# Sparse gate weights by accumulating scatters instead of one-hot products, and finer steps for attention units and scan chunks

## Chip, cores and metric

The kernel runs on one core of one Trainium2 chip. The metric is the device time of one execution in microseconds (us); most executions of this kernel agree within 0.3%. The engines are named as the profile names them: PE (matrix products; PEld is its loading of weights), DVE (vector), ACT (scalar), POOL (GpSimd, which here issues the indirect DMAs) and SP (which here issues nearly all other DMAs).

## What is computed

One layer of a hybrid decoder on 1024 tokens of width 1024, in float32. The mixer has three branches (a chunked state-space scan, dilated attention in three groups of heads, attention into 256 memory tokens), each gated and merged. Then comes the part that the change is about, a retrieval of single-neuron experts:

```
top, pos = top_k(cand, 16)               # per token: 8 heads x 16 = 128 of 16384 experts
idx  = take_along_axis(cidx, pos)
gate = softmax(top)                      # 128 gates per token
act  = gelu(einsum('bld,blhkd->blhk', hn, expert_down[idx]))
coef = gate * act
h   += einsum('blhk,blhkd->bld', coef, expert_up[idx])
```

## The kernel before, in words

**Stages.** The tokens are worked on in two halves of 512 (four tiles of 128). Each half runs `front` (scan, attention, gated merging), `close` and `route` (which chooses each token's experts). The second half's `front` and `close` run from about 1300 to 2250 us, and the stage in which the dense tiles' products are made (the `product` stage of `dense`) runs from about 2391 us to the end.

**Two ways through the experts.** Tiles 0, 1, 4 and 5 are gathered: for each of a token's 128 experts an indirect DMA brings one row of `in_down_dram` for each of 128 tokens (`dots`, tile `rowd`, L1141; DVE multiplies it with the token, L1135), and later one row of `in_up_dram` (`ups`, tile `rowu`, L1194; PE sums four such rows at once, L1180). All indirect DMAs stand in POOL's queue. Tiles 2, 3, 6 and 7 are dense: all 16384 experts are computed for them, and the gates of those that were not chosen are zero. So a dense tile needs a table of 128 tokens by 16384 gates. `gates_of` makes it: for each four tokens, DVE compares the expert numbers with a row of 0 to 127, once for the upper 7 bits and once for the lower 7 (L1256, L1257), ACT scales one of the two one-hot matrices by the gates (L1259), PE multiplies the two (`s<-work,work`, 128x128), ACT copies the result out of PSUM (L1235), and SP writes it to the DRAM tensor `w_park` (L1238). `load_gates` (L1345) reads the table back, into `wbig`, while the product stage runs.

**What sets the order.** `main` is a generator of PE blocks. Beside it run the `sides`: generators of the retrieval (heads, dots, ups, and for tiles 2 and 3 `early_gates`), each of which goes one step when a clock of estimated PE time (`pe_us`) reaches its due time, and says how much later its next step is due (2.31 for a dot, 4.4 for an up row, 4 for a step of `early_gates`). In the second half's `front`, `early_gates` is begun after `dil_close`. Within `main`, `par` runs two generators side by side by weights: attention units (`unit`) and scan chunks (`ssd_scan`) have weight 4, the projections beside them 8 to 34, and one whole unit or chunk is one step. After that a scheduler sets the order of the instructions on each engine, which is not the order in which they were written.

**Names.** `work` and `slab` are 128x512 tiles in SBUF, `t`, `s`, `mm` and `up` tiles in PSUM, `whi` and `wlo` the upper and lower part of a weight block, `coef` and `g` hidden activations of the dense tiles.

Of the kernel before, what the change touches and what calls it, by code (L numbers as in the profile page):

```python
# [91 lines left out]
D1, D2, D3, U1, U3, U4, H1, H3, L1, L2, L3, L4, WG = 2.31, 4.4, 4.4, 4.4, 4.4, 1.76, 3.0, 5.43, 9, 4.3, 2.52, 5, 4  # L92
# [12 lines left out]
def tile_hybrid_block(ctx: ExitStack, tc: tile.TileContext, keep_d, cst_d, vec_d, row_d, pos_d, xT_d, memT_d, w_in, w_mem_kv,  # L105
# [455 lines left out]
    def ssd_scan(hf, g, dts, proj):  # L561
# [4 lines left out]
        for c in range(NT):  # L566
# [24 lines left out]
            nc.vector.tensor_tensor(out=L3, in0=L3, in1=btok[:, 128:256].unsqueeze(1).to_broadcast([P, 4, P]), op=ALU.mult)  # L591
            yp = ps(tag)
# [107 lines left out]
    def unit(hf, g, i, qT, st):  # L700

        blocks = [kv[hf, g, i]]
# [25 lines left out]
        pT = []  # L728
        for hp in range(2):
            for hh in range(2):  # L730
                h = 2 * hh + hp
                x = pr[hp][:, hh * 256:hh * 256 + nk]
                nc.scalar.activation(out=x, in_=x, func=AF.Exp, scale=0.125, bias=nm[:, h:h + 1], accum_out=st[:, 260 + h:261 + h])
            tp = ps()
# [6 lines left out]
            pT.append(dst)  # L741
        op = ps()
# [26 lines left out]
    def dil_units(hf, g, qT, other):  # L769
# [4 lines left out]
        for i in range(NT):  # L774
            unit(hf, g, i, qT, st[i])
# [18 lines left out]
    def dil_close(hf, qT, nat):  # L794
# [3 lines left out]
        for n in range(NT):  # L798
            a = work(width=264)
            unit(hf, 0, n, qT, a)  # L800
# [408 lines left out]
    w_park = dram.tile([P // KG, P, NB, KG, WT], F32, name="w_park")  # L1209

    def gates_of(d, expert, gate, alloc, ps, hot, stage_of, both=None):
# [17 lines left out]
        def product():  # L1229
# [6 lines left out]
            if t4 == WT // 4 - 1:  # L1236
                for c0, n, part in stage:
                    nc.sync.dma_start(w_park[c0 // KG:(c0 + n) // KG, :, d * (P // WT) + b].rearrange("g p k t -> p g (k t)"),  # L1238
# [27 lines left out]
    def dense(hn, dpool):  # L1266
# [78 lines left out]
        def load_gates(c):  # L1345
# [48 lines left out]
    def ssd(hf, u, last):  # L1394

        dts, proj = yield from chain(ssd_dt(hf, u), ssd_proj(hf, u, 0))
        for g in range(4):
            beside = (ssd_proj(hf, u, g + 1), 12) if g < 3 else last
            _, proj = yield from par((ssd_scan(hf, g, dts, proj), 4), beside)
        return proj  # L1400

    def attend(hf, u, mp, *more):
# [3 lines left out]
        st, q2 = yield from par((dil_units(hf, 1, q1, None), 4), (dil_project(hf, u, 2), 16))  # L1406
        _, got = yield from par((dil_units(hf, 2, q2, st), 4), (chain(dil_project(hf, u, 0), *more), MORE))
# [8 lines left out]
    def front(hf, u, before):  # L1416
# [21 lines left out]
    def early_gates():  # L1438
        def stage_of(b):
# [98 lines left out]
```

## Time and profile before

| | us |
| --- | --- |
| time before, median of 3 runs | 3897.52 (3895.51 to 3899.34) |
| the profiled execution's own time | 3877.24 |
| its span in the trace | 3875.4 |
| PE busy | 3654.6 (94%) |
| DVE busy | 2747.3 (71%) |
| ACT busy | 1497.7 (39%) |
| POOL busy | 1178.7 (30%) |

The profiled execution is 20.3 us shorter than the median of the timed runs, and 1.8 us of it lie outside the span. Issuing a DMA is counted as busy on POOL (the indirect DMAs, whose addresses it works out) and not on SP.

### The profile page before, as it was taken

How to read it: one execution, taken by the hardware profiler on the slowest of the kernel's cores; microseconds unless marked ns; L12 is line 12 of the kernel's file. 1: busy time of each engine (PE TensorE's matmuls, PEld its weight loads, DVE VectorE, ACT ScalarE, POOL GpSimd, SP SyncE). 2: the span in 40 equal slices, each digit the busy share in tenths (PEclk: the TensorE clock that was granted, in tenths of full speed). 3: DMA queues.
4: the chain of work that ended last, by engine and by line, in shares of the span. 5: the costliest groups of instructions: out<-in, count | busy, mean ns of one | idle time of the engine just before them, and what ended most of it. 6: DMA issues, size and time to landing. Idle time of an engine off the chain costs nothing. (4 is left out here: it accounts for less than half of the span.)

```text
span 3875.4 us, 53775 instructions
## 1 busy us (share of the span) xinstructions
PE 3654.6 (94%) x17696; PEld 2759.9 (71%) x17696; DVE 2747.3 (71%) x7067; ACT 1497.7 (39%) x3326; POOL 1178.7 (30%) x1081
## 2 busy tenths in 40 slices
PE   8989999999989898999898888999999999999997
PEld 5767888876766686766666666777777777777664
DVE  5764555458999879988669998986666666666432
ACT  4444444343443333555542574232223222222221
POOL 0000000000024433434244412554443344444444
PEclk9989999999999978999899999999999999999999
DMA  3223334444457767888798878998988889899997
GB/s 98 73 80 112 99 108 120 128 152 136 112 194 237 262 192 244 285 302 308 248 337 316 314 252 313 351 345 329 328 320 317 284 325 329 319 323 320 332 334 293
DMA packets 459287, 956.27 MB, mean 247 GB/s; under 512 B 46336, under 2 KB 172032, under 8 KB 459008
## 3 DMA queue, kind: packets, MB, share of 16 engines
q0 software_dynamic: 147456, 536.94, 38.8%
q1 hardware_dynamic: 311552, 415.91, 32.9%
q8 instruction: 139, 2.28, 0.2%
q14 instruction: 140, 1.15, 0.1%
HBM read 882.94 MB, written 69.73 MB: 246 GB/s over the span
## 5 line engine op out<-in xcount | busy, mean ns | idle before, releaser
L246 ACT CAST whi<-wraw 128x512 fp32r<-128x512 f32 (+2 forms) x802 | 489.9, 611 | 1233.1 <-PE mm L174 879.3
L1141 POOL DMA_INDIRECT rowd<-in_down_dram,ids x512 | 595.1, 1162 | 1070.6 <-DVE act L1135 696.2
L247 DVE TENSOR_TENSOR wlo<-wraw,whi 128x512 fp32r<-128x512 f32 (+2 forms) x802 | 540.4, 676 | 490.6 <-ACT whi L246 455.0
L174 PE MATMUL mm<-uslab,whi 128*128 128x512 f32 x2240 | 738.3, 407 | 7.1 <-ACT whi L246 2.8
L1194 POOL DMA_INDIRECT rowu<-in_up_dram,ids x448 | 498.8, 1113 | 642.1 <-PE up L1180 506.1
L174 PE MATMUL mm<-whi,coef 128*128 128x512 f32 x2048 | 672.8, 399 | 5.5 <-DVE acc L1390 5.5
L174 PE MATMUL s<-uslab,whi 128*128 128x512 f32 (+1 forms) x2080 | 656.9, 397 | 10.4 <-ACT whi L246 4.1
L1135 DVE CUSTOM_DVE_ANT_0 rowd<-rowd,rowd 128x1024 f32<-128x1024 f32 x512 | 615.4, 1217 | 35.3 <-DMA rowd<-in_down_dram,ids 35.0
L174 PEld LDWEIGHTS mm<-uslab,whi 128*128 128x128 f32 x2240 | 419.9, 192 | 101.9 <-issue 11.6
L174 PEld LDWEIGHTS s<-uslab,whi 128*128 128x128 f32 (+1 forms) x2080 | 387.7, 189 | 129.9 <-issue 33.3
L174 PEld LDWEIGHTS mm<-whi,coef 128*128 128x128 f32 x2048 | 387.9, 189 | 126.4 <-issue 22.5
L174 PE MATMUL mm<-uslab,wlo 128*128 128x512 f32 x1120 | 451.6, 405 | 6.5 <-DVE wlo L247 6.4
L174 PE MATMUL s<-uslab,wlo 128*128 128x512 f32 (+1 forms) x1040 | 412.5, 397 | 13.9 <-DVE wlo L247 13.9
L174 PE MATMUL mm<-wlo,coef 128*128 128x512 f32 x1024 | 406.4, 397 | 3.8 <-DVE wlo L247 3.8
L247 DVE TENSOR_TENSOR wlo<-coef,whi 128x512 fp32r<-128x512 f32 x200 | 138.0, 690 | 224.1 <-ACT whi L246 220.1
L246 ACT CAST whi<-coef 128x512 fp32r<-128x512 f32 x200 | 124.2, 621 | 381.2 <-PE s L174 308.4
L174 PE MATMUL mm<-slab,whi 128*128 128x512 f32 x768 | 253.6, 409 | 6.3 <-DVE slab L247 2.7
L174 PEld LDWEIGHTS mm<-uslab,wlo 128*128 128x128 f32 x1120 | 213.6, 191 | 60.6 <-DVE wlo L247 10.2
L174 PEld LDWEIGHTS s<-uslab,wlo 128*128 128x128 f32 (+1 forms) x1040 | 196.0, 188 | 63.3 <-DVE wlo L247 17.9
L536 POOL COPY slab<-halo 128x3 f32<-128x3 f32 x32 | 14.7, 465 | 737.4 <-PE mm L174 723.2
L174 PEld LDWEIGHTS mm<-wlo,coef 128*128 128x128 f32 x1024 | 194.3, 190 | 48.1 <-DVE wlo L247 4.2
L1180 PE MATMUL up<-rowu,one_col 128*32 128x512 f32 x1792 | 220.0, 600 | 0.6 <-DVE one_col L1177 0.6
(318 smaller groups left out, 5279.9 us busy)
## 6 DMA issues: line engine op xcount, KB each, us to landing
wraw<-in_up_dram SPq DMA_DIRECT2D x256, 256.0 KB
coef<-in_downT_dram SPq DMA_DIRECT2D x200, 256.0 KB
wraw<-in_w_in_dram SPq DMA_DIRECT2D x152, 256.0 KB
wbig<-w_park SPq DMA_DIRECT2D x128, 256.0 KB
wraw<-in_w_in_dram SPq DMA_DIRECT2D x160, 128.0 KB
slab<-y_park SPq DMA_DIRECT2D x64, 256.0 KB
wraw<-in_w_query_dram SPq DMA_DIRECT2D x64, 256.0 KB
w_park<-work SPq DMA_DIRECT2D x64, 256.0 KB
```

Source lines behind the costliest of these rows:

```text
L174: return nc.tensor.matmul(o, lhsT, rhs, **kw)
L246: nc.scalar.copy(hi, src)
L247: nc.vector.tensor_tensor(out=lo, in0=src, in1=hi.bitcast(F32), op=ALU.subtract)
L536: nc.gpsimd.tensor_copy(r[:, 0:3], halo[:, f, :])
L1135: pinned(nc.vector.tensor_tensor_reduce(out=r, in0=r, in1=hn, scale=1.0, scalar=0.0, op0=ALU.mult, op1=ALU.add, accum_out=act[:, j:j + 1]))
L1141: nc.gpsimd.indirect_dma_start(out=r, out_offset=None, in_=down_d, in_offset=bass.IndirectOffsetOnAxis(ap=ids[:, j:j + 1], axis=0))
L1180: pinned(nc.tensor.matmul(up[32 * q:32 * q + 32, hh * 512:(hh + 1) * 512], z[:, q, 31 - n:63 - n], four[q][:, hh * 512:(hh + 1) * 512], st ...
L1194: nc.gpsimd.indirect_dma_start(out=r, out_offset=None, in_=up_d, in_offset=bass.IndirectOffsetOnAxis(ap=ids[:, 128 + t:129 + t], axis=0))
```

## The change

**Gates of tiles 2 and 3.** The one-hot products of these two tiles go. In their place are two DRAM tensors, `w_early0` and `w_early1`, of 128 x 16384 floats each. `zeros` fills them in the first half with 32 DMA writes of 512 KB on SP, from a buffer that POOL sets to zero. `scatter` turns each token's expert numbers into addresses (nine small DVE instructions for a tile; `token_place` makes the token's part once) and issues 128 indirect DMAs on POOL for each tile (L1258 of the kernel after); each adds 128 gates of 4 bytes, one for each token, to the zeroed tensor. `early_gates` of a tile is now a side that begins when the tile is routed. `load_gates` reads half of each `wbig` row group from `w_early0` and `w_early1`, after whatever scatters are left have been written out in the program. Tiles 6 and 7 keep the one-hot products.

**Steps.** `unit` and `ssd_scan` yield three times where they yielded once, and their weight in `par` goes from 4 to 12, so a third of a unit now stands where a whole one stood.

```
 def unit(hf, g, i, qT, st):
...
         nc.vector.tensor_scalar(out=nm, in0=st[:, 256:260], scalar1=-0.125, scalar2=None, op0=ALU.mult)
-        pT = []
         for hp in range(2):
...
                 nc.scalar.activation(out=x, in_=x, func=AF.Exp, scale=0.125, bias=nm[:, h:h + 1], accum_out=st[:, 260 + h:261 + h])
+        yield
+        pT = []
+        for hp in range(2):
             tp = ps()
...
             pT.append(dst)
+        yield
         op = ps()
...
-            unit(hf, g, i, qT, st[i])
+            yield from unit(hf, g, i, qT, st[i])
...
-    w_park = dram.tile([P // KG, P, NB, KG, WT], F32, name="w_park")
+    NE = NB // 2
+    w_park = dram.tile([P // KG, P, NB - NE, KG, WT], F32, name="w_park")
+    w_early = [dram.tile([P * P * P, 1], F32, name=f"w_early{d}") for d in range(NA)]
+
+    def zeros():
+        z = row4("rowu", NU_BUFS)
+        nc.gpsimd.memset(z, 0.0)
+        for w in w_early:
+            for part in w.rearrange("(n p f) o -> n p (f o)", p=P, f=D):
+                nc.sync.dma_start(part, z)
+                yield paces["zeros"]
...
+    def scatter(d, expert, gate):
...
+        ids = expert.bitcast(I32)
+        nc.vector.tensor_copy(ids, a)
+        for k in range(P):
+            nc.gpsimd.indirect_dma_start(out=w_early[d], out_offset=bass.IndirectOffsetOnAxis(ap=ids[:, k:k + 1], axis=0),
+                                         in_=gate[:, k:k + 1], in_offset=None, compute_op=ALU.add)
+            yield paces["scatter"]
...
-            last_w[0] = nc.sync.dma_start(wbig[n % 2][:, at:at + NB // KG], w_park[n, :, at:at + NB // KG])
-
+            if at < NE:
+                d, b = divmod(at, NE // NA)
+                w = w_early[d].rearrange("(n p b k t) o -> n p b k (t o)", p=P, b=NE // NA, k=KG, t=WT)
+            else:
+                w, b = w_park, at - NE
+            last_w[0] = nc.sync.dma_start(wbig[n % 2][:, at:at + NB // KG], w[n, :, b:b + NB // KG])
+
+        for job in early:
+            for _ in job:
+                pass
...
-            _, proj = yield from par((ssd_scan(hf, g, dts, proj), 4), beside)
+            _, proj = yield from par((ssd_scan(hf, g, dts, proj), 12), beside)
...
-        yield from par((dil_close(hf, q0, nat), 4), (gated(hf, u, 0, 2, merged), 14))
+        yield from par((dil_close(hf, q0, nat), 12), (gated(hf, u, 0, 2, merged), 14))
         if hf:
-            early.append(early_gates())
             paces.update(later=L2)
-            sides.append([early[0], pe_us[0]])
...
-    def early_gates():
...
+    def early_gates(tt):
+        while tt not in routed:
+            yield IDLE
+        yield from scatter(DENSE.index(tt), *routed[tt])
...
         sides.append([gathers(queue, dots, "dots"), pe_us[0]])
         sides.append([gathers(ready, ups, "ups"), pe_us[0]])
+        for tt in DENSE:
+            if tt < NT:
+                early.append(early_gates(tt))
+                sides.append([early[-1], pe_us[0]])
```

**POOL's queue in the second half.** In the kernel before, this stretch of the queue holds gathers alone: `rowd` rows for `dots`, `rowu` rows for `ups`.

```order
L1141 DMA rowd_3710_16489<-in_down_dram,ids_2289_10288 128x1024 [waits DMASW4_49,DVE_49]
L1141 DMA rowd_3727_16578<-in_down_dram,ids_2289_10288 128x1024 [waits DMASW5_49,DVE_49]
L1194 DMA rowu_3728_16590<-in_up_dram,ids_2196_9872 128x1024 [waits DMASW6_49,PE_49]
L1194 DMA rowu_3729_16592<-in_up_dram,ids_2196_9872 128x1024 [waits DMASW7_49,PE_49]
L1141 DMA rowd_3736_16620<-in_down_dram,ids_2289_10288 128x1024 [waits DMASW0_49,DVE_49]
L1194 DMA rowu_3743_16651<-in_up_dram,ids_2196_9872 128x1024 [waits DMASW1_49,PE_49]
L1194 DMA rowu_3767_16732<-in_up_dram,ids_2196_9872 128x1024 [waits DMASW2_49,PE_49]
```

Afterwards the scatters of both tiles stand between them (the next eleven rows; `gate` is the tile that is added, `expert` now holds the addresses, and a second DMASW name in the brackets is the landing of the scatter before into the same tensor).

```order
L1258 DMA w_early0_146<-gate_3219_14342,expert_2291_10318 2097152x1 [waits DMASW4_49]
L1258 DMA w_early1_147<-gate_3672_16373,expert_3221_14349 2097152x1 [waits DMASW5_49]
L1147 DMA rowd_3766_16772<-in_down_dram,ids_2289_10313 128x1024 [waits DMASW6_49,DVE_49]
L1258 DMA w_early0_146<-gate_3219_14342,expert_2291_10318 2097152x1 [waits DMASW7_49,DMASW4_49]
L1258 DMA w_early1_147<-gate_3672_16373,expert_3221_14349 2097152x1 [waits DMASW5_49,DMASW0_49]
L1147 DMA rowd_3772_16797<-in_down_dram,ids_2289_10313 128x1024 [waits DMASW1_49,DVE_49]
L1200 DMA rowu_3741_16666<-in_up_dram,ids_2197_9900 128x1024 [waits DMASW2_49,PE_49]
L1200 DMA rowu_3754_16721<-in_up_dram,ids_2197_9900 128x1024 [waits DMASW3_49,PE_49]
L1200 DMA rowu_3760_16746<-in_up_dram,ids_2197_9900 128x1024 [waits PE_49]
L1200 DMA rowu_3773_16800<-in_up_dram,ids_2197_9900 128x1024 [waits PE_49]
L1258 DMA w_early0_146<-gate_3219_14342,expert_2291_10318 2097152x1 [waits DMASW7_49,DMASW6_49]
```

From the first scatter to the last, POOL's queue now holds 505 indirect DMAs, 256 scatters and 249 gathers. Of the 254 scatters that follow one into the same tensor, 44 stand directly behind it in the queue, 75 have one other DMA between, 70 two, 16 three, and 49 four or more.

What moved: as many gathers as before stand in the stretch, within a dozen, and 256 scatters have come in between them, each but the first two behind a landing.

**SP's queue where the gates are first read.** In the kernel before, the first loads of the product stage (L1350) stand among weight loads, behind the writes of tiles 6 and 7 (L1238).

```order
L1238 DMA w_park_145<-wbig_4390_19444 128x16x128 [waits DMAHW3_49,Activation_49]
L1289 DMA wraw_4843_22107<-in_downT_dram 128x512 [waits DMAHW4_49,DVE_49]
...
L1289 DMA wraw_4856_22164<-in_downT_dram 128x512 [waits DMAHW6_49,DVE_49]
L1350 DMA wbig_4875_22250<-w_park_145 128x512 [waits DMAHW7_49,PE_49]
L1350 DMA wbig_4875_22250<-w_park_145 128x512 [waits DMAHW0_49]
L1238 DMA w_park_145<-wbig_4390_19444 128x16x128 [waits DMAHW1_49,Activation_49]
```

Afterwards the first load that reads `w_early1` waits for the last scatter (DMASW6), and behind it in the same queue stand the loads of parked hidden blocks (L1359) and of up weights (L1437).

```order
L1437 DMA wraw_4656_21492<-in_up_dram 128x512 [waits DMAHW2_49,DVE_49]
L1092 DMA sc_4979_22931<-sc_park_140 128x512 [waits DMAHW6_49,DMAHW0_49,DVE_49]
L1406 DMA wbig_4606_21282<-w_early1_147 128x512 [waits DMASW6_49]
...
L1406 DMA wbig_4611_21295<-w_early1_147 128x512 [waits DMAHW4_49]
L1359 DMA g_4734_21836<-g_park_18289 128x512 [waits DMAHW5_49,DVE_49]
...
L1359 DMA g_4784_22079<-g_park_18289 128x512 [waits DMAHW0_49,DVE_49]
L1406 DMA wbig_4724_21801<-w_early0_146 128x512 [waits DMAHW2_49,DMAHW1_49,DVE_49]
L1437 DMA wraw_4659_21510<-in_up_dram 128x512 [waits DVE_49]
```

What moved: the gate loads that the product stage begins with stood behind SP's own writes, and stand now behind POOL's queue of scatters, through that one wait.

**PE's queue in an attention unit of the second half.** Before, the products of one unit's end (`t<-slab,work`, the values) stand eight rows behind the transposes of its probabilities (`t<-keep,work`), with transposes of something else (`s<-keep,slab`) between them here and there.

```order
L174 MATMUL mm_3010_13406<-uslab_1942_8516,wlo_3059_13641 128x512
L178 MATMUL t_2983_13312<-keep_87,work_2978_13292 128x128 [waits PE_49,Activation_49]
...
L178 MATMUL s_2985_13321<-keep_87,work_2979_13293 128x128 [waits PE_49,Activation_49]
...
L174 MATMUL t_2987_13328<-slab_2680_11940,work_2984_13317 128x64 [waits DVE_49,Activation_49]
L174 MATMUL t_2987_13328<-slab_2866_12746,work_2984_13317 128x64 [waits DMAHW5_49]
L178 MATMUL s_2996_13369<-keep_87,slab_2937_13080 128x128 [waits DVE_49,PE_49]
L178 MATMUL s_2996_13369<-keep_87,slab_2939_13085 128x128
```

Afterwards the two kinds stand a little further apart, and the transposes of the projection are in one piece between them.

```order
L174 MATMUL mm_3010_13427<-uslab_1945_8560,wlo_3062_13685 128x512
L178 MATMUL t_2991_13377<-keep_87,work_2981_13336 128x128 [waits PE_49,Activation_49]
...
L178 MATMUL s_2993_13384<-keep_87,work_2982_13337 128x128 [waits PE_49,Activation_49]
...
L178 MATMUL t_3000_13404<-keep_87,slab_2936_13098 128x128 [waits DVE_49]
...
L178 MATMUL s_3002_13411<-keep_87,slab_2936_13098 128x128 [waits DVE_49]
...
L174 MATMUL t_3015_13449<-slab_2683_11984,work_2992_13382 128x64 [waits Activation_49]
L174 MATMUL t_3015_13449<-slab_2869_12790,work_2992_13382 128x64 [waits DMAHW6_49]
```

What moved: little; in either kernel other work stood between a unit's steps already, and the values come some sixteen rows behind the probabilities' transposes where it was eight.

Elsewhere PE loses the 256 products `s<-work,work` of tiles 2 and 3 and six transposes; DVE loses 128 comparisons of 128x512 and gets some twenty small instructions; ACT loses 256 scalings and 256 copies; SP loses 64 writes of 256 KB to `w_park` and gets the 32 writes of zeros, all among its first 110 DMAs, seven of them in a row. The number of gate loads stays 128, of which 64 now read `w_early0` and `w_early1`.

## Rows read from the trace of the kernel before

**Rows 1.** The page: busy time of each engine, share of the span, instructions.

```profile
PE 3654.6 (94%) x17696; PEld 2759.9 (71%) x17696; DVE 2747.3 (71%) x7067; ACT 1497.7 (39%) x3326; POOL 1178.7 (30%) x1081
```

**Rows 2.** Stretches: length, each engine's busy time (instructions), clock, DMA share, GB/s.

```profile
0.00:100.00 100.00, 81.12 (x348) 57.56 (x349) 54.32 (x126) 42.45 (x80) 5.65 (x18) 0.93 0.37 97
100.00:200.00 100.00, 99.98 (x478) 76.36 (x477) 72.89 (x162) 49.30 (x102) 6.20 (x18) 1.00 0.29 74
200.00:300.00 100.00, 86.02 (x397) 68.31 (x397) 65.68 (x170) 47.38 (x115) 2.19 (x5) 0.81 0.31 91
1556.00:2391.00 835.00, 742.78 (x3862) 561.71 (x3860) 705.92 (x2072) 432.39 (x1203) 306.04 (x261) 0.95 0.86 297
2391.00:3600.00 1209.00, 1203.45 (x5627) 901.44 (x5626) 854.64 (x1605) 350.19 (x590) 541.38 (x486) 1.00 0.90 325
3600.00:3875.00 275.00, 248.03 (x1316) 160.40 (x1314) 97.36 (x175) 53.76 (x91) 128.12 (x129) 0.96 0.86 316
```

**Rows 3.** Groups of instructions, 1600 to 2000 us: busy, mean ns | idle before, releasers.

```profile
L1259 ACT ACTIVATE work<-work,work 128x128 f32<-128x128 f32 x256 | 84.3, 399 | 64.6 <-DVE work L1257 57.0 <-DVE posf L1028 5.9 <-ACT work L1235 1.5
...
L174 PE MATMUL s<-work,work 128*128 128x128 f32 x512 | 80.2, 299 | 27.0 <-ACT work L1259 27.0
...
L1257 DVE TENSOR_TENSOR work<-keep,work 128x512 f32<-128x512 f32 x64 | 43.8, 684 | 21.3 <-DMA w_park<-work 19.7 <-ACT work L1235 1.6
L1256 DVE TENSOR_TENSOR work<-keep,work 128x512 f32<-128x512 f32 x64 | 43.7, 683 | 10.8 <-DMA w_park<-work 7.0 <-DMA h_park<-work 3.8
```

**Rows 4.** POOL alone, groups of instructions from 1556 to 2391 us, same columns.

```profile
L1194 POOL DMA_INDIRECT rowu<-in_up_dram,ids x140 | 163.4, 1167 | 263.0 <-PE up L1180 219.7 <-issue 24.4 <-DVE expert L1034 7.3
L1141 POOL DMA_INDIRECT rowd<-in_down_dram,ids x121 | 142.7, 1179 | 266.3 <-DVE act L1135 187.7 <-DVE vals L991 22.0 <-issue 8.8
```

**Rows 5.** POOL's waits, 1556 to 2391 us: waited for, us in total, times, longest.

```profile
POOL rowu L1194 <- PE up L1180: 219.7, 23, 38.1
POOL rowd L1141 <- DVE act L1135: 187.7, 46, 13.7
POOL rowu L1194 <- issue: 24.4, 80, 0.3
...
POOL rowd L1141 <- issue: 8.8, 29, 0.3
```

**Rows 6.** One line's instructions, L1141: the gathers of dots.

```profile
L1141 POOL DMA_INDIRECT rowd<-in_down_dram,ids x512: 932/948/3215, 1043.0 to 3599.8; - x171
...
DMA to landing us min/median/max: 4.1/6.6/11.9
```

**Rows 7.** The same view of L1194, the gathers of ups.

```profile
DMA to landing us min/median/max: 4.1/7.2/12.8
```

**Rows 8.** The page: DMA queues, packets, MB, share of 16 engines' span.

```profile
q0 software_dynamic: 147456, 536.94, 38.8%
```

**Rows 9.** PE's waits over the whole span: waited for, us in total, times, longest.

```profile
PE up L1180 <- DMA rowd<-in_up_dram,ids: 22.0, 5, 10.4
...
PE t L178 <- ACT work L733: 7.5, 1, 7.5
PE s L178 <- ACT work L733: 7.5, 6, 5.3
...
PE s L174 <- ACT work L584: 3.7, 2, 2.3
...
PE t L178 <- DVE work L599: 3.0, 2, 2.0
...
PE s L178 <- DVE work L599: 2.3, 3, 1.0
...
PE t L174 <- ACT work L584: 1.5, 1, 1.5
```

**Rows 10.** The chain that ended last, its last rows: start, us, what it was.

```profile
3859.80 1.35 POOLq L1534
3861.15 0.30 issue
3861.46 5.44 DMA rowd<-in_up_dram,ids
3866.89 0.14 issue
```

More of the change, by code (lines that the diff above doesn't have):

```diff
@@ L91 @@
 EVAC = 168
[L92 removed]
+D1, D2, D3, U1, U3, U4, H1, H3, L1, L2, L3, L4, WS, ZP = 2.31, 4.4, 4.4, 4.4, 4.4, 1.76, 3.0, 5.43, 9, 4.3, 2.52, 5, 4, 20
 ND_BUFS, NU_BUFS = 5, 8
@@ L741, in unit @@
             pT.append(dst)
+        yield
         op = ps()
@@ L799, in dil_close @@
             a = work(width=264)
-            unit(hf, 0, n, qT, a)
+            yield from unit(hf, 0, n, qT, a)
             join(a, nat[n])
@@ new lines, in tile_hybrid_block, with token_place @@
+    at_token = rows4.tile([P, 1], F32, name="at_token")
+    def token_place():
+        j = new(small, [P, 16, NCAND], F32, "junk", 1).rearrange("p a b -> p (a b)")
+        nc.vector.tensor_tensor_reduce(out=j[:, 0:P], in0=ident, in1=iota, scale=1.0, scalar=0.0, op0=ALU.mult, op1=ALU.add,
+                                       accum_out=j[:, P:P + 1])
+        ei = gtiny(P, I32, "ei", 1)
+        nc.vector.tensor_copy(ei[:, 0:1], j[:, P:P + 1])
+        nc.vector.tensor_scalar(out=ei[:, 0:1], in0=ei[:, 0:1], scalar1=4, scalar2=None, op0=ALU.logical_shift_right)
+        nc.vector.tensor_copy(at_token, ei[:, 0:1])
+        nc.vector.scalar_tensor_tensor(at_token, at_token, float(KG * WT - WT), j[:, P:P + 1], op0=ALU.mult, op1=ALU.add)
@@ L1237, in product @@
                 for c0, n, part in stage:
-                    nc.sync.dma_start(w_park[c0 // KG:(c0 + n) // KG, :, d * (P // WT) + b].rearrange("g p k t -> p g (k t)"),
+                    nc.sync.dma_start(w_park[c0 // KG:(c0 + n) // KG, :, d * (P // WT) + b - NE].rearrange("g p k t -> p g (k t)"),
                                       part.rearrange("p (g k) t -> p g (k t)", k=KG))
@@ L1405, in attend @@
         _, q1 = yield from par((mem_units(hf, 1, mp), 6), (dil_project(hf, u, 1), 16))
-        st, q2 = yield from par((dil_units(hf, 1, q1, None), 4), (dil_project(hf, u, 2), 16))
-        _, got = yield from par((dil_units(hf, 2, q2, st), 4), (chain(dil_project(hf, u, 0), *more), MORE))
+        st, q2 = yield from par((dil_units(hf, 1, q1, None), 12), (dil_project(hf, u, 2), 16))
+        _, got = yield from par((dil_units(hf, 2, q2, st), 12), (chain(dil_project(hf, u, 0), *more), MORE))
         return got[0], dil_order(st)
@@ L1436, in tile_hybrid_block @@
     sides = []
-    def early_gates():
-        def stage_of(b):
-            return [(32 * k, 32, work().rearrange("p (c t) -> p c t", t=WT)) for k in range(4)]
-        for d, tt in enumerate(DENSE):
-            if tt < NT:
-                while tt not in routed:
-                    yield IDLE
-                for _ in gates_of(d, *routed[tt], work, ps, lambda n: work(), stage_of):
-                    yield paces["gates"]
+    def early_gates(tt):
+        while tt not in routed:
+            yield IDLE
+        yield from scatter(DENSE.index(tt), *routed[tt])
     def gathers(todo, job, pace):
@@ L1458, in main @@
         u = split_u(norm_u(xT_d, 0, HB, V_MIX))
+        token_place()
+        paces.update(zeros=ZP)
+        sides.append([zeros(), pe_us[0]])
         merged = yield from front(0, u, [mem_prepare()])
@@ L1462, in main @@
         xs = []
-        paces.update(dots=D1, ups=U1, heads=H1, later=L1, gates=WG)
+        paces.update(dots=D1, ups=U1, heads=H1, later=L1, scatter=WS)
         sides.append([heads(*HEADS_A), pe_us[0]])
@@ L1474, in main @@
             next(sides[0][0])
-        for _ in early[0]:
-            pass
         sides.append([heads(*HEADS_B), pe_us[0]])
```

12 lines of the change are left out of this document (added).

## The prediction

> **What bounds the kernel now.** I read the page first: PE is busy for 94% of the span, DVE for 71%, ACT for 39%, POOL for 30% [rows 1]. Such a share is a mean over stages, so the stretches come next [rows 2]. In the product stage (2391 to 3600 us) PE works 1203 of 1209 us; nothing but fewer products can shorten it, and the change removes none there. The stretch before it, 1556 to 2391 us, holds the second half's attention, its merging, and the gates of tiles 2 and 3. PE works 743 of its 835 us, DVE 706, and POOL only 306, in 261 gathers. The reader is to see two things in it: PE sets its length, and POOL, which the change loads most, is the engine with most room. Whether that room is enough is the question, and it is asked of time in POOL's queue and not of busy time: POOL stood still in this stretch chiefly because buffers were not yet free (219.7 us on PE's sums, 187.7 us on DVE's dots) [rows 5].
>
> **What leaves the path.** The groups of 1600 to 2000 us hold the whole of the old gates [rows 3]: the one-hot products keep PE busy for 80.2 us, and PE stood idle for 27.0 us in front of them until ACT had scaled (six transposes are under 2 us more). With their 107 us plus 2 gone, PE would need 835 - 109 = 726 us for this stretch. The comparisons (43.7 + 43.8 us of DVE) and the scalings (84.3 us of ACT) go too. They lay beside PE's work, so I count them at nothing, and what hides them is PE itself; where DVE is late, it is late for other work and gains from this.
>
> **What comes in on POOL.** Between the first and the last scatter POOL's queue holds 505 indirect DMAs, 256 of them scatters. One gather keeps POOL busy for 1.17 us, as the mean of either kind [rows 4], and 0.30 us of issue come before one that waited for nothing else (24.4 us in 80 times, 8.8 in 29) [rows 5]: 1.47 us, and 505 of them make 742 us. The median gather is shorter, 948 ns [rows 6]; with it the queue would need 505 x 1.25 = 631 us. No scatter stands in the trace; it makes 128 addresses as a gather does, so these are its two bounds, and I take the mean, since the same stretch gave it. So already without a wait POOL needs 742 us where PE needs 726. POOL's new work is no longer hidden; it is the stretch.
>
> **The wait that is new.** A scatter waits until the scatter before into the same tensor has landed. Queued behind it on POOL are the gathers, and DVE's dots and PE's sums wait for those; in PE's own order the sums stand between projections, so PE stops with them. At the end the first gate load waits for the last scatter, and SP's queue behind it holds the loads of parked hidden blocks and up weights, so the product stage cannot begin earlier either. How long is a landing (L, from issue)? The gathers land in 4.1 us at least and 6.6 and 7.2 us at the median [rows 6, 7]. A gather moves 512 KB: 1024 of them took 38.8% of the 16 engines' span [rows 8], which is 0.388 x 3875.4 / 1024 = 1.47 us each. A scatter moves 512 bytes, so I take that away: L lies between 4.1 - 1.5 = 2.6 us and about 7.5 - 1.5 = 6 us. The chain's end also shows a gather with nothing of POOL's behind it: 5.44 us, then 0.14 us until the waiting engine started [rows 10]. I take 3.4 us, the lower end and half a gather's 1.47 us, because a scatter mostly finds one gather of its own queue still moving, and the stretch's DMA share will fall from 0.86 [rows 2] when POOL slows the gathers. That choice is the weakest in this sum.
>
> With m other DMAs between two scatters of one tensor, the wait is L + 0.14 - 1.47 (m + 1), if that is above zero. Of the 254 pairs 44 have m = 0, 75 m = 1, 70 m = 2, 16 m = 3. L = 2.6 gives 44 x 1.27 = 56 us. L = 3.4 gives 44 x 2.07 + 75 x 0.60 = 136 us. L = 4.5 gives 44 x 3.17 + 75 x 1.70 + 70 x 0.23 = 283 us. L = 6 gives 44 x 4.67 + 75 x 3.20 + 70 x 1.73 + 16 x 0.26 = 571 us. So the stretch, 835 us before, takes 798, 878, 1025 or 1313 us; at L = 3.1 it breaks even. For my value: 878 - 835 = +43 us.
>
> Such a wait could be thought shorter still. The Trainium skill, "DMA: Bandwidth & Descriptors", section "Anatomy of one DMA — SWDGE (gpsimd) path", gives a DMA of this queue a fixed part of about 2.0 us and little else for so few bytes. By it, L = 2.0 would leave 44 x 0.67 = 29 us of waits, and the time would be about 3830 us. No row here shows so little: 4.1 us less 1.5 is 2.6 [rows 6, 8]. The same page's "Rules for kernel authors" speaks against the change: under 64 KB a transfer is mostly overhead.
>
> **Finer steps.** In the whole span PE waits 15.0 us for ACT's exponentials and transposed probabilities' copies (L733), 5.2 us for L584 and 5.3 us for L599 of the scan [rows 9], 25.5 us together. Finer steps can take away at most these, and could as well put a new wait in; PE's order moves by a few rows at such a place. Bounds: -25.5 to about +5 us. I take -20, nearer to the rows' sum, since projections now come between. Half belongs to the second half of the tokens, whose stretch POOL now sets, so there it returns nothing: -10 us.
>
> **Zeros.** 32 writes of 512 KB stand among SP's first 110 DMAs, in some 200 us whose DMA share is 0.29 to 0.37 [rows 2]. At 1.47 us of all engines each they are 47 us of transfer, hidden by that room, except where seven stand in a row ahead of weight loads: 7 x 1.47 = 10 us. Bounds 0 and 10; I take 7, since PE already has a gap in that stage (81 of the first 100 us busy) and no spare weights to cover one. The 64 writes of 256 KB to `w_park` that go are as many bytes, in the stretch that POOL now sets: nothing. The nine address instructions per tile, on DVE, and the gate loads from another tensor: nothing, covered by DVE's idle fifth of the stretch and by five hidden blocks ahead of the first product.
>
> **Sum.** +43 - 10 + 7 = +40 us on the profiled 3877.2, which is 3917; the median of the runs is 20.3 us above the profile, and I keep that distance: 3897.5 + 40 = 3937 us.
>
> **Rivals.**
>
> *Landings are short or POOL is quick.* For it: POOL's median duration, and a scatter has hardly any bytes. Against it: DMA share 0.86 in the stretch, and a landing floor of 4.1 us. With L = 2.6 the stretch is 798 us: -37 - 3 = -40, so 3857 us. With the median 1.25 us of POOL too, POOL needs 631 + 44 x 1.49 + 75 x 0.24 = 715 us, less than PE's 726, and the whole gain arrives: -109 - 20 + 7 = -122, so 3775 us. It decides below L = 3.1.
>
> *Landings as long as the gathers'.* The scatters stand in the same queue as the gathers, and if they land no sooner than what was issued ahead of them, L nears 6: +478 - 3, so about 4370 us; it decides from L = 4.6, where the time passes 4090 us. Against it: much of the gathers' median is their own bytes, and with POOL waiting fewer DMAs are in flight.
>
> *Nothing changes.* Gain and wait cancel near L = 3.1: 3890 to 3905 us.
>
> **How the numbers follow.** Forecast case (POOL's queue ends last, L between 3.1 and 4.6): 0.46, its own range 3905 to 4090 us. Short landings: 0.38 (3775 to 3890). Cancelling: 0.08. Long landings: 0.08. A difference under 0.2%, some 8 us, is about what a measurement of this kernel cannot tell from none; so faster 0.38, same 0.08, slower 0.54. The range leaves out the long landings and the lowest tenth of the cases, where POOL's median and short landings meet: 3795 to 4090 us.
>
> **What would show it.** In the profile after: POOL's rows for the scatter line give its duration (1.0 to 1.2 us expected) and its landing (3.4); POOL's waits should name the scatters themselves with 100 to 200 us, and PE's waits should show the sums (`up<-rowu`) or DVE's dots waiting for gathers, which hardly occurred. The stretch up to the first product should be about 878 us long with PE busy for some 660. If PE is busy for 95% of it, POOL was never late, and the rival of short landings holds. If the first 300 us are longer by more than 10 us, the zeros were under-priced; if PE's waits for L733, L584 and L599 stay at 25 us, the finer steps did nothing. I would be wrong above all if a scatter's landing isn't near 3.4 us.

## The result: 7% slower, and the profile after

The kernel after takes 4173.0 us (median; 4160.8 to 4179.3) against 3898.4 us beside it, a ratio of 1.0699 with an interval of 1.0674 to 1.0724. The forecast was 3937 us with a range of 3795 to 4090: slower was right (0.54 had been put on it), the size was not, and the range was too short.

The page of the profile says at once that no engine works longer on the whole, except POOL (after, to be held against [rows 1]; the second line shows PE in 40 equal slices of the span, in tenths):

```profile
PE 3649.3 (87%) x17178; PEld 2735.8 (66%) x17178; DVE 2677.3 (64%) x6955; ACT 1379.2 (33%) x2812; POOL 1605.3 (38%) x1338
...
PE   8989999999988988777876753399999999999997
```

PE has 3649 us of work in a span of 4174 instead of 3655 in 3875. Its new idle time lies in slices 17 to 26. The stretches show it (columns as in [rows 2]; first the stretch that took 835 us before, by the clock, then the same up to the last scatter):

```profile
1556.00:2391.00 835.00, 625.44 (x2849) 457.65 (x2847) 528.96 (x1688) 242.37 (x506) 584.18 (x408) 0.86 0.74 220
1556.00:2665.00 1109.00, 733.03 (x3388) 539.38 (x3386) 686.65 (x2250) 322.64 (x715) 740.96 (x509) 0.81 0.70 205
```

To compare like with like I cut both profiles at the same weight blocks (the casts `whi<-wraw` on ACT, of which there are 802 in every kernel here; the 326th, 376th and 551st). The part up to the 326th takes 1201 us before and 1198 after. From there to the 376th it is 310 and 335 us, from there to the 551st, where the product stage begins, 880 and 1146 us, and the rest of the span 1484 and 1496 us. Before rounding the differences are -3.0 + 24.5 + 265.4 + 12.1 = 299.0, which is the difference of the spans. Nearly all of the loss lies in the stretch that the prediction named.

What POOL does there (groups of POOL from 1556 to 2665 us, to be held against [rows 4]; then POOL's own waits in it):

```profile
L1258 POOL DMA_INDIRECT w_early<-gate,expert x256 | 457.1, 1785 | 279.6 <-DMA w_early<-gate,expert 218.4 <-issue 53.4 <-ACT work L753 7.6
L1147 POOL DMA_INDIRECT rowd<-in_down_dram,ids x125 | 143.1, 1145 | 50.4 <-issue 26.2 <-DVE work L766 6.9 <-DVE act L1141 6.2
L1200 POOL DMA_INDIRECT rowu<-in_up_dram,ids x128 | 140.8, 1100 | 39.0 <-issue 29.3 <-PE mm L174 4.3 <-PE s L174 2.1
```

```profile
POOL w_early L1258 <- DMA w_early<-gate,expert: 218.4, 107, 6.4
POOL w_early L1258 <- issue: 53.4, 147, 4.3
...
POOL rowd L1147 <- DVE act L1141: 6.2, 5, 2.8
...
POOL rowu L1200 <- PE up L1186: 1.5, 5, 0.3
```

POOL is busy for 457 + 143 + 141 = 741 of the 1109 us, waits 218 us for the landings of its own scatters, and 109 us (53.4 + 26.2 + 29.3) are issue. So 1068 us are the queue's own, and it hardly ever waits for a buffer (6.2 us for DVE's dots and 1.5 for PE's sums, where [rows 5] had 187.7 and 219.7). In the 835 us before, busy time and issue made 339 us [rows 4, 5]. With the idle time before them, the 253 gathers take (143.1 + 50.4 + 140.8 + 39.0) / 253 = 1.475 us each; the prediction had 1.47. The 256 scatters take (457.1 + 279.6) / 256 = 2.88 us each; the prediction had 1.47 and 136 / 256 = 0.53 of waits, 2.00 together.

Who waits for POOL (waits of DVE and of PE, 1556 to 2700 us):

```profile
DVE rowd L1141 <- DMA rowd<-in_down_dram,ids: 299.1, 57, 27.3
DVE g L1421 <- DMA wbig<-w_early: 38.4, 1, 38.4
```

```profile
PE mm L174 <- ACT coef L246: 84.6, 1, 84.6
PE mm L174 <- DVE wlo L247: 58.5, 13, 14.7
PE mm L174 <- ACT wbig L1310: 50.4, 26, 15.6
PE s L174 <- DVE wlo L247: 44.5, 15, 12.7
PE up L1186 <- DMA rowu<-in_up_dram,ids: 33.1, 2, 25.8
PE mm L174 <- DVE slab L963: 29.5, 1, 29.5
```

DVE stands 299 us in front of dots whose gather is late (35.0 in the whole span before, in the trace's view of DVE's waits). PE's waits then name DVE and ACT (`wlo`, `wbig`), since the splits of weights and the one-hot work of tiles 6 and 7 stand behind those dots in DVE's queue: of the 29.5 us for `slab` and the 14.7 us for `wlo`, DVE itself stood 23.2 and 12.5 us in front of a dot whose gather was late. The longest wait, 84.6 us, is at the end: the first product, behind the last scatters.

How long a landing takes is seen in the chain of waits there (start, us, what), first where gathers move as well, then among the last 17 scatters, which follow one another with nothing between:

```profile
2589.96 7.55 DMA w_early<-gate,expert
...
2602.47 3.40 DMA w_early<-gate,expert
...
2606.32 3.90 DMA w_early<-gate,expert
...
2652.21 2.91 DMA w_early<-gate,expert
2655.12 0.27 issue
2655.39 3.01 DMA w_early<-gate,expert
...
2661.84 3.06 DMA w_early<-gate,expert
2664.90 0.02 issue
2664.91 0.33 SPq L1406
2665.24 0.05 issue
2665.29 3.56 DMA wbig<-w_early
```

Alone, in the last dozen, a scatter lands 2.9 to 3.1 us after its issue (counted from the start of its instruction on POOL). Where gathers move it takes longer, up to 7.55 us in this piece of the chain. Since a chain picks out the longest, I took all 107 waits for landings from the trace: 42 of the 44 pairs with nothing between wait, and before 2600 us their landings (26) have a median of 4.2 us. With one DMA between, 39 wait, at a median of 4.7 us; there only the late ones show. The longest landing is 11.0 us. The chain goes on from the last scatter (2661.84) to SP's gate load, to DVE, and to the first product at 2670 us.

### The profile page after: what moved, and what is told of

It is laid out like the page before. It is cut to its first block, busy times and chain, and to the rows that moved or that the text cites. A ratio compares the mean times of both kernels' runs of the same rounds, so it can differ in the third digit from the quotient of the medians.

```text
span 4174.5 us, 52179 instructions
## 1 busy us (share of the span) xinstructions
PE 3649.3 (87%) x17178; PEld 2735.8 (66%) x17178; DVE 2677.3 (64%) x6955; ACT 1379.2 (33%) x2812; POOL 1605.3 (38%) x1338
## 4 chain that ended last, share of the span: by engine, by line
PE 67%; DMA 11%; DVE 8%; issue 7%; POOL 6%; ACT 1%; SPq 0%; POOLq 0%; DVEq 0%; another core or an unknown queue 0%; ACTq 0%
PE mm L174 40%; PE s L174 18%; DMA w_early<-gate,expert 5%; PE up L1186 5%; DMA rowd<-in_down_dram,ids 4%; PE t L174 3%; POOL w_early L1258 3%; POOL rowu L1200 2%; DVE rowd L1141 2%; POOL rowd L1147 1%; DVE wlo L247 1%; DMA rowd<-in_up_dram,ids 1%; PE s L178 1%; PE t L178 1%; DVE junk L1039 0%
## 5 line engine op out<-in xcount | busy, mean ns | idle before, releaser
L1147 POOL DMA_INDIRECT rowd<-in_down_dram,ids x512 | 584.3, 1141 | 871.6 <-DVE act L1141 562.0
L1141 DVE CUSTOM_DVE_ANT_0 rowd<-rowd,rowd 128x1024 f32<-128x1024 f32 x512 | 616.5, 1219 | 334.4 <-DMA rowd<-in_down_dram,ids 334.1
L174 PE MATMUL mm<-whi,coef 128*128 128x512 f32 x2048 | 673.0, 398 | 93.3 <-ACT coef L246 84.6
L174 PE MATMUL s<-uslab,whi 128*128 128x512 f32 (+1 forms) x2080 | 667.6, 403 | 5.1 <-DVE uslab L247 2.8
L1200 POOL DMA_INDIRECT rowu<-in_up_dram,ids x448 | 478.1, 1067 | 440.1 <-PE up L1186 321.0
L1258 POOL DMA_INDIRECT w_early<-gate,expert x256 | 457.1, 1785 | 279.6 <-DMA w_early<-gate,expert 218.4
L174 PE MATMUL mm<-slab,whi 128*128 128x512 f32 x768 | 257.4, 416 | 51.5 <-DVE slab L963 29.5
```

The source lines that it names most:

```text
L174: return nc.tensor.matmul(o, lhsT, rhs, **kw)
L1141: pinned(nc.vector.tensor_tensor_reduce(out=r, in0=r, in1=hn, scale=1.0, scalar=0.0, op0=ALU.mult, op1=ALU.add, accum_out=act[:, j:j + 1]))
L1147: nc.gpsimd.indirect_dma_start(out=r, out_offset=None, in_=down_d, in_offset=bass.IndirectOffsetOnAxis(ap=ids[:, j:j + 1], axis=0))
L1200: nc.gpsimd.indirect_dma_start(out=r, out_offset=None, in_=up_d, in_offset=bass.IndirectOffsetOnAxis(ap=ids[:, 128 + t:129 + t], axis=0))
L1258: nc.gpsimd.indirect_dma_start(out=w_early[d], out_offset=bass.IndirectOffsetOnAxis(ap=ids[:, k:k + 1], axis=0), in_=gate[:, k:k + 1], in_ ...
```

## Experiments

The theory: the scatters fill POOL's queue, by their own time and by their landings, and everything that waits for gathers waits with it. The rivals: the finer steps cost; the zeros or the other gate loads cost; the landings alone make the loss, or POOL's time alone. Times are medians, and ratios are to the kernel before on the same chip.

**Finer steps alone.** The kernel before, with this and the yields in `unit` and `ssd_scan`:

```
-            _, proj = yield from par((ssd_scan(hf, g, dts, proj), 4), beside)
+            _, proj = yield from par((ssd_scan(hf, g, dts, proj), 12), beside)
-        st, q2 = yield from par((dil_units(hf, 1, q1, None), 4), (dil_project(hf, u, 2), 16))
+        st, q2 = yield from par((dil_units(hf, 1, q1, None), 12), (dil_project(hf, u, 2), 16))
```

> The kernel before with the finer steps alone (three steps in unit and ssd_scan, weights 12); the gates stay one-hot products. Theory (POOL's queue of scatters sets the stretch, the steps do little): 3878 to 3905 us, between the 20 us that the prediction gave them and nothing, since the first half of the kernel after came to the same marks within 1 us. Rival (the finer steps are what costs): above 4000 us, PE idle around the attention units.

Measured: 3911.8 us, ratio 1.0027 (1.0014 to 1.0040). The steps do not make the 7%, and they do not give the 10 to 20 us either that the prediction had from them; they cost some 10 us. Where, the windows of the 25 weight blocks from the 326th on show (before; with finer steps):

```profile
1201.00:1340.00 139.00, 124.05 (x575) 93.30 (x573) 121.83 (x341) 50.02 (x116) 59.19 (x46) 0.98 0.77 247
```

```profile
1199.00:1358.00 159.00, 131.56 (x583) 98.14 (x582) 131.06 (x385) 48.42 (x112) 55.92 (x49) 0.92 0.71 227
```

159 us instead of 139, with DVE busy for 131 instead of 122 and PE idle for 27 instead of 15 us. These blocks hold the end of the second half's scan and the attention into the memory tokens. (The second half's `front` begins earlier than the 1300 us named above: before, the lines of `ssd_scan` run there from 986 to 1241 us, those of `mem_units` from 1234 to 1323.) Of the 20 us some 10 come at the scan's end (1224 to 1259 us with finer steps) and 7 in the attention behind it (1304 to 1335). PE's longest wait is for DVE in both places, 6.9 us for `wlo` and 5.6 us for a tile of `mem_units`, while DVE also works on the first half's dots.

**Scatters without finer steps.** The kernel after, with one step for a unit or chunk:

```
-            _, proj = yield from par((ssd_scan(hf, g, dts, proj), 12), beside)
+            _, proj = yield from par((ssd_scan(hf, g, dts, proj), 4), beside)
```

> The kernel after with units and chunks in one step and weight 4 again; zeros and scatters stay. Theory (the scatters alone make the loss): 4150 to 4200 us. Rival (finer steps, or their meeting with the scatters): 3900 to 4050 us.

Measured: 4156.5 us, ratio 1.0664 (1.0642 to 1.0685). The theory holds; the 16 us below the kernel after are near the steps' own price, some 10 us.

**No scatters.**

```
-        for k in range(P):
-            nc.gpsimd.indirect_dma_start(out=w_early[d], ...)
-            yield paces["scatter"]
+        yield IDLE
```

> The kernel after without its 256 scatters; zeros, address arithmetic, gate loads from the zeroed tensors and finer steps stay, so the gates of tiles 2 and 3 are left out of the result. Theory (only the scatters on POOL cost, the rest of the change gains): PE loses 109 us of the stretch and nothing takes their place, so 3898 - 109 = 3789, range 3770 to 3810 us. Rival (the zeros, the other gate loads or the steps cost as well): above 3830 us.

Measured: 3834.7 us, ratio 0.9849 (0.9825 to 0.9873). So the scatters cost 4173 - 3835 = 338 us, and all else together gains 64 us, not 109. The rival's bound (3830) is just passed. Of the missing 45 us the steps explain some 10. The stretch from the 376th to the 551st block explains the most of the others (with finer steps alone; without scatters):

```profile
1537.00:2426.00 889.00, 793.46 (x4098) 599.17 (x4100) 747.80 (x2216) 449.21 (x1247) 314.63 (x271) 0.95 0.85 290
```

```profile
1529.00:2332.00 803.00, 714.44 (x3536) 536.26 (x3535) 672.65 (x2093) 331.45 (x733) 310.34 (x260) 0.95 0.85 292
```

889 becomes 803 us, 86 less (the two runs' medians differ by 77). PE's work falls by 79 us, as the 80.2 of [rows 3] promised. PE's idle time falls by 7 us alone (95.5 to 88.6), where the 27.0 us in front of the one-hot products had been counted as gone: other waits took their place (in these two stretches `mm` for ACT's `wbig` went from 15.7 to 26.1 us, and 15.6 us for DVE's `slab` are new). The zeros leave no trace: the first 326 blocks take 1198 us with them and 1201 without.

The same part of the kernel after shows how PE lost the time that the scatters cost:

```profile
1533.00:2678.00 1145.00, 763.65 (x3523) 563.49 (x3522) 716.66 (x2320) 333.60 (x734) 748.59 (x515) 0.82 0.70 206
```

Of 342 us more (1145 - 803) PE is idle for 293 and busy for 49, with as many products. The 49 us go with the granted clock, 0.82 on average instead of 0.95: during and just behind PE's waits it stands at the lower of its two levels (0.5, which is 1.2 GHz), as from 2589 to 2674 us, around the wait of 84.6 us that ends at 2670.

**No landing waits.**

```
-            nc.gpsimd.indirect_dma_start(out=w_early[d], ...
+            nc.gpsimd.indirect_dma_start(out=w_early[d] if k % 8 == 0 else w_other[d][k % 8 - 1], ...
```

> The kernel after with the scatters of a tile spread over eight DRAM tensors in turn, of which one is read, so that no scatter waits for the one before; the gates of seven in eight scatters are left out of the result. POOL's busy time in the stretch was 741 us, its waits for landings 218 of 1109 us. If both POOL's time per scatter (1.79 us) and the waits count: 4173 - 218 = 3955, range 3920 to 3990 us. If the waits alone made the loss: 3790 to 3830 us, as without scatters. If the scatters' own time on POOL alone did, or other waits come in the place of these: 4100 us or more.

Measured: 4113.0 us, ratio 1.0549 (1.0529 to 1.0570). With no waits for landings only 60 us come back, not 218, so they are not the whole loss, and what I expected of both together fell too; what holds is the last case, 4100 us or more. The scheduler had moved the scatters closer together: they stand in POOL's queue from 1576 to 2325 us, with 161 gathers between where there were 249, so the order is not that of the kernel after. The groups of POOL from 1556 us on show that a scatter that waits for nothing still takes 1.72 us and 0.30 of issue:

```profile
L1260 POOL DMA_INDIRECT w_other<-gate,expert x224 | 384.7, 1717 | 68.3 <-issue 63.7 <-DMA w_other<-gate,expert 3.0 <-DMA w_early<-gate,expert 0.9
```

From 1556 to 2325 us POOL's busy time (617.7) and issue (111.5) make 729 of 769 us: POOL is nearly full again, only earlier, and PE works 490 of the 769 us.

**Writes instead of additions.** The order of every queue stays.

```
-                                         in_=gate[:, k:k + 1], in_offset=None, compute_op=ALU.add)
+                                         in_=gate[:, k:k + 1], in_offset=None)
```

> The kernel after with scatters that write instead of add (the order of every queue stays the same; where two heads of a token chose one expert, one gate is left out). Theory (a scatter's time on POOL, 1.59 us at the median, and its landing belong to scattering 4-byte pieces and not to the addition): 4160 to 4190 us, with 1.5 to 1.6 us of POOL for each. Rival (the addition is what is dear): POOL near a gather's 0.94 us and a shorter landing, 256 x 0.65 = 166 us and more off, 3900 to 4010 us.

Measured: 4063.6 us, ratio 1.0415 (1.0390 to 1.0440), 109 us less. My theory of this run fell, and the rival's cause holds (the addition is dear), though not its size (166 us and more). One line's instructions, with additions (kernel after) and with writes; durations are min/median/max in ns:

```profile
L1258 POOL DMA_INDIRECT w_early<-gate,expert x256: 1552/1594/6077, 1578.2 to 2661.8; - x128
```

```profile
L1258 POOL DMA_INDIRECT w_early<-gate,expert x256: 963/1001/3584, 1579.3 to 2559.1; - x128
```

A scatter that writes takes 1.0 us of POOL, like a gather (948 ns in [rows 6]); one that adds takes 1.59. In the stretch POOL's scatters now sum to 312.5 + 318.5 = 631 us instead of 737 (the landing waits rose from 218 to 255 us):

```profile
L1258 POOL DMA_INDIRECT w_early<-gate,expert x256 | 312.5, 1221 | 318.5 <-DMA w_early<-gate,expert 254.7 <-issue 52.2 <-ACT work L753 7.5
```

The scatters are busy for 145 us less and wait 36 us more for landings: 106 us less in POOL's queue, 109 us less time. With the order unchanged, the sum of POOL's queue is the time here. A landing is shorter, too, when the scatter writes: 2.1 us among the last of them, where those that add had 2.9 to 3.1 (pieces of the chain of waits of this run):

```profile
2554.32 2.14 DMA w_early<-gate,expert
...
2556.74 2.13 DMA w_early<-gate,expert
...
2559.14 2.15 DMA w_early<-gate,expert
```

**Half of the scatters.**

```
-        for k in range(P):
+        for k in range(0, P, 2):
```

> The kernel after with every second scatter left out, 64 of 128 for each tile, at twice the pace (half of these gates are left out of the result). Theory (POOL's queue is the bound only while its sum is above PE's need of about 803 us, as measured without scatters): 249 x 1.475 + 128 x 2.05 = 630 us of POOL plus some 100 us of waits stay below it, so 3835 to 3880 us. Rival (each scatter costs wherever it stands, since it delays the gathers behind it): half way between 3835 and 4173, 3980 to 4030 us.

Measured: 3978.0 us, ratio 1.0202 (1.0177 to 1.0227). My theory fell here as well (the rival's range begins 2 us higher): POOL's sum over the stretch (528.5 us busy, 73.9 of issue and 132.2 of landings, 735 together) lies below what PE needs (803), and still the kernel is slower than before. The two windows tell why, the one in which scatters are queued and the one behind it up to the first product:

```profile
1577.00:2247.00 670.00, 518.25 (x2333) 375.27 (x2332) 434.06 (x1376) 182.44 (x349) 432.66 (x311) 0.87 0.75 233
2247.00:2474.00 227.00, 187.81 (x970) 148.20 (x969) 197.99 (x570) 131.06 (x340) 84.38 (x67) 0.88 0.89 300
```

The groups of POOL in the first window:

```profile
L1258 POOL DMA_INDIRECT w_early<-gate,expert x127 | 223.6, 1761 | 163.4 <-DMA w_early<-gate,expert 132.2 <-issue 23.7 <-ACT work L753 7.6
L1147 POOL DMA_INDIRECT rowd<-in_down_dram,ids x92 | 107.1, 1164 | 53.4 <-DVE act L1141 21.7 <-issue 17.7 <-DMA w_early<-gate,expert 4.0
L1200 POOL DMA_INDIRECT rowu<-in_up_dram,ids x92 | 102.3, 1112 | 28.0 <-issue 21.3 <-PE mm L174 3.7 <-PE s L174 2.1
```

Busy time (433 us), issue (63) and landings (136) make 632 of 670 us: while scatters stand in it, the queue is nearly full, and PE works 77% of the window (89% of the stretch without scatters). Later POOL has room (busy for 84 of 227 us), and what PE lost is not made up. A sum is to be taken over the window in which the new work is queued, not over the stage.

**One tile by scatters, one by products.** This could have beaten both kernels; steps are as before.

```
+        if d == 0:
+            yield from scatter(d, *routed[tt])
+        else:
+            for _ in gates_of(d, *routed[tt], work, ps, lambda n: work(), stage_of):
+                yield paces["gates"]
```

> One tile by scatters (tile 2), tile 3 by one-hot products as in the kernel before, and units and chunks in one step as before; the result is complete. Theory: POOL's sum is that of the run with half of the scatters, PE saves half of the 86 us that the gates gave, 3898 - 43 = 3855, range 3835 to 3875 us. Rival (one chain of 128 landings into one tensor, some 6 us each under load, stands in the way of the gathers between): 3900 to 4000 us.

Measured: 4001.3 us, ratio 1.0253 (1.0225 to 1.0281). The rival holds (its range ended 1 us lower). With one tensor alone most scatters meet the landing of the one before: 225.8 us in 91 waits, more than 256 scatters had in two tensors (218.4).

```profile
L1258 POOL DMA_INDIRECT w_early<-gate,expert x128 | 237.9, 1859 | 242.2 <-DMA w_early<-gate,expert 225.8 <-issue 16.1 <-DMA rowu<-in_up_dram,ids 0.3
```

**Up rows put off.**

```
-D1, D2, D3, U1, U3, ... = 2.31, 4.4, 4.4, 4.4, 4.4, ...
+D1, D2, D3, U1, U3, ... = 2.31, 4.4, 4.4, 13.2, 3.3, ...
```

> The run with scatters and without finer steps, with up rows due every 13.2 instead of 4.4 in the second half's front and every 3.3 instead of 4.4 later: 40 of 128 up gathers leave POOL's queue between the first and the last scatter. Theory (POOL's sum sets the stretch): 4157 - 40 x 1.475 = 4098 us, range 4085 to 4125 us. Rival (the landing chain of the scatters alone sets it, gathers fill its gaps): 4150 to 4165 us, or more if the rows that were put off come late at the end.

Measured: 4147.3 us, ratio 1.0628 (1.0602 to 1.0654). Between the two forecasts: the part from the 376th to the 551st block fell from 1148 to 1107 us, by 41 of the 59 us that 40 gathers fewer were to give, and the part behind it rose from 1495 to 1531 us, where the rows came later. Moving gathers out of the way gains some 9 us here.

**Neither additions nor landing waits.** Both edits together.

> The run without landing waits (eight tensors in turn, one of them read, seven in eight gates left out), with writes in place of additions: POOL's queue order is that run's, and each scatter costs POOL its 1.0 us and 0.28 us of issue and nothing else. Theory (what a scatter takes of POOL's time is the loss, through the gathers behind it): while scatters were queued that run gave POOL 256 x 2.0 + 166 x 1.475 = 757 us of work in 769 us; now it is 256 x 1.28 + 166 x 1.475 = 573 us, so POOL has room again and the time falls by about 184 us from 4113, to 3930, range 3850 to 3960 us. Rival (it is the memory traffic or the delay of single gathers that costs, not POOL's time): 4060 to 4115 us.

Measured: 4018.8 us, ratio 1.0289 (1.0262 to 1.0317). Neither forecast holds: 94 us less than with additions, not 184. In this profile POOL waits for buffers again (37.8 and 18.6 us from 1560 to 2250), but ACT and DVE stand for up to 27 and 25 us in front of work for which the trace shows no cause:

```profile
ACT whi L246 <- remote: 84.7, 12, 26.7
ACT whi L246 <- issue: 81.9, 21, 26.2
```

These waits come with the writes: while scatters are queued, ACT has 38 us of these two kinds in the kernel after and 98 in the run with writes (same order of every queue), 35 in the run without landing waits and 218 us in 690 in this one (same order again). The longest stand where many scatters follow one another with no gather between. These windows (columns as in [rows 2]) hold 24 and 26 of them:

```profile
1850.00:1879.00 29.00, 9.58 (x16) 3.83 (x16) 0.69 (x1) 0.62 (x1) 21.99 (x24) 0.59 0.14 48
1983.00:2015.00 32.00, 7.50 (x35) 3.29 (x33) 3.18 (x5) 1.14 (x3) 24.38 (x26) 0.64 0.15 47
```

DVE and ACT all but stand still for 29 and 32 us, PE works 10 and 8 of them, and the DMA engines are busy for 14 and 15%. With additions the same 24 and 26 scatters took 47 us each, PE worked 20 and 19 of them, and no wait of this kind was as long (13.6 us at the most on ACT). Why the engines stand is open. So this run, with no waits for landings and POOL's busy time and issue at 580 of 673 us, still loses 184 us (4019 - 3835) against the run without scatters: for scatters that write and do not wait, POOL's time is not shown to be the whole of the loss.

**The scan's steps alone, and the units' steps alone,** each in the kernel before:

```
+            _, proj = yield from par((ssd_scan(hf, g, dts, proj), 12), beside)
```

> The kernel before with the scan's finer steps alone (three steps in ssd_scan, weight 12). With all finer steps the kernel ran 10.5 us longer, and in every profile that has them the 25 weight blocks from 1200 us on took 159 to 161 us against 139 to 140 without; the second half's scan is done there. Theory (the scan's steps cost these 20 us, the attention's give a part back): 3908 to 3920 us, with the 20 us in the same place. Rival (the attention's steps cost): 3893 to 3903 us.

```
+        st, q2 = yield from par((dil_units(hf, 1, q1, None), 12), (dil_project(hf, u, 2), 16))
```

> The kernel before with the attention units' finer steps alone. Theory (the scan's steps cost 20 us, the units' give 5 to 10 back): 3885 to 3898 us, and the 25 weight blocks from 1200 us on take 140 us as before. Rival (the units' steps cost): 3905 to 3915 us.

Measured: 3911.7 us, ratio 1.0026 (1.0011 to 1.0040), and 3905.5 us, ratio 1.0013 (0.9999 to 1.0027). The 25 blocks from the 326th on take 162 us with the scan's steps and 139 with the units':

```profile
1195.00:1357.00 162.00, 133.24 (x582) 99.14 (x583) 134.05 (x391) 48.66 (x112) 56.96 (x51) 0.92 0.71 227
```

```profile
1199.00:1338.00 139.00, 125.16 (x575) 94.38 (x573) 122.44 (x343) 50.03 (x116) 59.60 (x46) 0.98 0.77 248
```

So the cost comes with the scan's steps and shows at the end of the second half's scan and behind it, where DVE also has the dots of the first; the units' steps make no difference that was measured, and the gain that I expected of them isn't there.

No version with scatters beat the kernel before: with half of them the loss is already 143 us over the run without any (3978 - 3835), and the whole gain to be had is 64. Scatters spread thinner over the span, or queued behind the gathers, were not tried.

## Why the prediction was wrong, step by step

**Right: the mechanism.** POOL's queue becomes the stage, DVE's dots and PE's sums wait for gathers behind it, and the first gate load waits for the last scatter. Each is in the profile after: 1068 of 1109 us are POOL's own, DVE waits 299 us, and at the end SP stands 57.5 us in front of the first gate load and PE 84.6 in front of the first product. A gather came to 1.475 us where 1.47 had been put, with some luck: it was busy for 1.12 us instead of 1.17, with 0.35 of idle time before it instead of 0.30.

**Wrong, and the most of it: a scatter's own time on POOL.** It was taken as a gather's mean, 1.17 us, with the gather's median as the other bound. It was 1.79 (median 1.59): 256 x 0.62 = 159 us. Both bounds came from gathers, so there was no bound above for a kind of DMA that the trace did not have, and the range was too short. That the addition makes the difference is shown by the run with writes (1.0 us, 109 us less time). By the prediction's own sum this price alone makes the stretch longer than before: 457 us busy, 53 of issue and 373 for the gathers are 884 us without any wait for a landing, against 835.

**Wrong: the landings, by half.** L was put at 3.4 us. Alone it was 2.9 to 3.1; under load it was 4.2 at the median where one scatter follows the other directly, between the value taken and the 6 us of the gathers' end. The waits were 218 us instead of 136; by the prediction's own formula L = 4.2 gives 44 x 2.87 + 75 x 1.40 = 231. Longer scatters leave less of a landing to wait for, and some landings were later than the median; these two were not taken apart. With both errors: (2.88 - 2.00) x 256 = 225 us, of the 1109 - 878 = 231 us by which POOL's sum was short. Each by itself (estimates by the prediction's sum): with L = 4.2 and the old price of a scatter 4033 us, inside the range; with the right price and 136 us of waits 4097, already above it.

The rival of short landings, at 0.38, did not come, and by the same sum the 884 us leave it no room. The Trainium skill, "DMA: Bandwidth & Descriptors", section "Anatomy of one DMA — SWDGE (gpsimd) path", gives a DMA of this queue a fixed part of about 2.0 us: the scatters that write come near it (2.1 us alone), those that add show 2.9 at the least, so for these the measurement decides against it. The rule of the same page of the Trainium skill, section "Rules for kernel authors", that transfers under 64 KB are mostly overhead, agrees: a scatter of 512 bytes cost POOL 2.88 us.

**Wrong: the sum over the stage.** The prediction compared POOL's sum with PE's need over the whole stretch, and the lower rival rested on that (POOL below 726 us, so the whole gain arrives). The run with half of the scatters shows that it is not enough.

**Wrong: what the removal gives.** 109 us were counted, 86 came in the stretch (77 by the medians). The products' 80.2 us were real. The 27.0 us of waiting in front of them went to other waits.

**Wrong: the finer steps.** -10 us was booked, +10.5 measured. The waits at L733, L584 and L599 [rows 9] were taken as an upper limit of the gain, with +5 as the worst; nothing in the rows spoke of how a finer mix meets DVE, which was busy for 122 of the 139 us where the cost came. Those waits stayed where they were: 25.6 us in the run with finer steps alone, 25.5 before, which was the sign named for steps that do nothing.

**Zeros.** +7 us booked; the runs show none.

**The sum, again.** In profiles: 299 us from one span to the other, of them 265 in the stretch, 25 at the end of the second half's scan and behind it, 12 in the product stage, and 3 less ahead of them. The medians differ by 275, since the profile of before was some 20 us under its median and that of after 3 above.

## What to carry to other kernels

An engine that is idle on average may be full while a new kind of work is queued on it: take the sum over that window, and price each piece by what queues behind it. For a kind of instruction that the trace doesn't have, a neighbour's durations were a lower bound here, and not both. And an idle row in front of work that is removed should be counted at nothing until the next-late thing is named.

## What was not expected of the hardware

- An indirect DMA that adds keeps POOL busy for 1594 ns at the median, one that writes the same pieces for 1001 ns.
- A scatter of 128 pieces of 4 bytes that adds lands 2.9 to 3.1 us after issue with nothing else in POOL's queue, one that writes after 2.1. While gathers move, directly following scatters that add had a median of 4.2 us.
- Scatters that write, without waits between them, came with stalls of up to 27 us on ACT and 25 us on DVE, the longest while 24 and 26 of them followed one another (218 us of such waits on ACT in all); with additions in the same order ACT had 35. No row shows why.
